# A three-part change to a hybrid decoder layer in fp32 on one core: 1/rms spread by its column, residual rows turned in a later stage by way of HBM, last partial products staged in working buffers

## The chip, the cores and the metric

The kernel runs on one core of a Trainium2 chip. The metric is the device time of one execution in microseconds (us); 843.92 is the median of three runs before the change. The engines are TensorE (PE; its weight loads are shown apart as PEld), VectorE (DVE), ScalarE (ACT), GpSimd (POOL) and SyncE (SP, which here only issues DMAs). Each engine works through its own instructions in the order in which the program holds them; an instruction that waits on a semaphore holds up all that stands behind it on its engine.

## What is computed

One layer: a half-step SwiGLU feed-forward block (FFN), a token mixer, and a second half-step FFN, each with RMSNorm before and after. There are 512 tokens of width 1024, and the FFN's hidden width is 2816 (22 chunks of 128). All is fp32.

```
x = x + 0.5 * rms_norm(swiglu(rms_norm(x, g1), w_gu1, w_down1), g1b)
x = x + rms_norm(hybrid_mixer(rms_norm(x, g2), ...), g2b)
x = x + 0.5 * rms_norm(swiglu(rms_norm(x, g3), w_gu2, w_down2), g3b)

rms_norm(x, g) = x * rsqrt(mean(x * x, -1) + 1e-6) * g
swiglu(x, w_gu, w_down): gate, up = split(x @ w_gu); (silu(gate) * up) @ w_down
```

The mixer joins a gated linear recurrence on half of its channels with sliding-window attention on the other half.

## The kernel before

**Products.** Every fp32 product is made of three: operands are split into a high part (rounded to the matmul's format, by ACT) and a low part (the rest, by DVE), and PE adds high x high, high x low and low x high. Weights go through the same split: a raw tile is loaded on SP's queue, ACT casts it (tiles whi...), DVE subtracts (wlo...). The class Weights does this a fixed number of units ahead of PE (AHEAD, 4), and its calls fix where the casts and subtractions stand in the order of ACT and DVE. `W.later(n, fn)` puts a step n units later.

**The residual stream** xT lies turned: features on the partitions, tokens along them, eight tiles of 128 x 512, in two raw buffers of 1 MB each out of five (NRAW). In the first FFN it is lent to HBM (`lend`, two DMAs of 1 MB on POOL's queue) and fetched back (`give_back`), so that the weights can have its buffers.

**1/rms.** At every RMSNorm the sums of squares are made by PE per half of 256 tokens (`InvRms.stats`, line 550), ACT takes the root (line 556), DVE the reciprocal (line 558): a column of 128 partitions x 2. `invert` then multiplies the identity by that column (dg, line 560, DVE), and `spread` (line 564) multiplies a matrix of ones with dg on PE, which gives 1/rms along the free dimension on all partitions. There are 12 such spreads.

**The second FFN** (loop over GROUPS2 at the end): chunks 0 to 5 are done in the plain way (`classic`); four octos follow, each for four chunks (f0 = 6, 10, 14, 18). `octo` makes gate and up with seven products instead of eight (the forms b11, t3, t2, b21, t1, t4, b22), each of 24 matmuls of 512 columns (line 951), in PSUM banks A, Dd and B, two banks each. The third form, t2, is added to A; the copies u2 (line 956) read A; the fifth, t1, is added to A again. The hidden values are turned by DVE into a tile z (line 961), put to HBM (h_b, line 965, SP's queue) and loaded again (hxb, line 1021, SP's queue) during the next octo, to serve as operands of `seven_down`. `seven_forms_of` hangs these steps on the products of the octo: its dictionary has step numbers as keys, where 1 is the loading of hxb and 2.5 the cast of its first block (line 827, ACT; low part line 834, DVE).

**seven_down** (line 1088 on) makes the down product of the previous octo's chunks, again in seven products (a11, s3, a12, s2, s4, a22, s1). From the second on, each ends in copies of two banks into stage tiles (line 1113, ACT) and accumulating DMAs of 256 KB on POOL's queue into HBM (yp_b, line 1116): 14 a group. A later accumulation to the same place waits until the earlier one has landed. The stage tiles are three acc tiles and one R tile, and then tiles of 2 KB a partition of the pool t2k (38 buffers).

**Pools.** wt gives working tiles (8 buffers), which an octo uses for p1, p7, u4 and its forms s1 to s4; wide gives tiles of 8 KB a partition (2 buffers), used for z and hxb.

**The rows.** The output is by tokens, so xT is turned back: `turn_back(c)` is one DVE transpose (in blocks of 32 x 32, line 1870) and four stores into x_hbm (line 1873, SP's queue), in runs of 32 floats. It runs eight times in `classic` of the second FFN, between the steps 2.5 and 4.5. The rows are loaded in the last group (read_x, line 1918).

Of the kernel before, what the change touches and what calls it, by code (L numbers as in the profile page):

```python
# [15 lines left out]
P = 128  # L16
# [106 lines left out]
def tile_layer(ctx: ExitStack, tc: tile.TileContext, out: bass.AP, **ins: bass.AP):  # L123
# [39 lines left out]
    def wt(name, w=T, dt=F32):  # L163
        return tmp.tile([P, w], dt, tag="w", name=name, bufs=NW)
# [304 lines left out]
    def filled(name, w, value):  # L469
        t = const.tile([P, w], F32, name=name)  # L470
        dve.memset(t, value)
        return t

    ones = filled("ones", P, 1.0)
    mean_d = filled("mean_d", 1, 1.0 / D)
    mean_c = filled("mean_c", 1, 1.0 / C)
    eps = filled("eps", 1, EPS)
# [61 lines left out]
    class InvRms:  # L539
# [13 lines left out]
        def invert(self, ms, scale=1.0):  # L553
            n = self.name
            rms = small.tile([P, 2], F32, tag="rms", name=f"rms_s{n}")
            act.activation(rms, ms, AF.Sqrt, bias=self.eps, scale=scale)
            rs = small.tile([P, 2], F32, tag="rs", name=f"rs_{n}")
            dve.reciprocal(rs, rms)
            self.dg = wt(f"dg_{n}", T)[:, :2 * P].rearrange("p (a b) -> p a b", a=2)
            dve.tensor_tensor(self.dg, ident.unsqueeze(1).to_broadcast([P, 2, P]), rs.unsqueeze(2).to_broadcast([P, 2, P]), op=ALU.mult)  # L560

        def spread(self):
            o = self.ps[:, T // 2:]
            pe.matmul(o, ones, self.dg.rearrange("p a b -> p (a b)"), start=True, stop=True)
            return o


# [231 lines left out]
    class Hidden:  # L799
# [129 lines left out]
            for j in range(2):  # L929
                self.hs[f + j] = hs[j]  # L930

        def octo(self, f, beside, soon=False):


            n = f"{self.name}{f}"

            def did(i):
                for fn in beside.get(i, ()):
                    fn()

            h_hbm = hbm.tile([4 * P, T], F32, name=f"h_{n}")

            def seven(b, form, first, i):
                for q in range(2):
                    hi, lo = W.take(3 if soon and i == 6 and q else AHEAD)
                    for tb in range(2):
                        blk = slice(tb * P, (tb + 1) * P)
                        for k in range(2):
                            xh, xl = self.nxt.t[form, 2 * q + k]
                            for j, (x, w) in enumerate(((xh, hi), (xl, hi), (xh, lo))):  # L950
                                pe.matmul(b[tb], x[:, blk], w[:, k, :], start=first and q + k + j == 0, stop=q + k == 2 and j == 2, skip_group_check=True)  # L951
                    did(i + q / 2)

            def each(fn, *args):
                for xs in zip(*args):
                    fn(*xs)

            def turned(xs, h):

                for tb, x in enumerate(xs):  # L960
                    dve.transpose(z.rearrange("p (j b n) -> p b j n", n=32, b=NB)[:, 2 * h + tb], x.rearrange("p (j n) -> p j n", n=32))

                def put():
                    for i in range(4):
                        sync.dma_start(h_hbm[:, i * P:(i + 1) * P].rearrange("(j a) n -> a j n", a=32), z[32 * i:32 * (i + 1)].rearrange("p (j n) -> p j n", n=P))

                if h:
                    W.later(1, put)

            def pair(make, name):  # L970
                return [make(f"{name}{n}{tb}") for tb in range(2)]

            z = wide(f"z{n}")
            A, Dd, B = (pair(bank, s) for s in "adb")
            p1, p7, u4 = (pair(wt, s) for s in ("p1", "p7", "u4"))
            u2 = pair(acc_tile, "u2")
            g1 = [acc_tile(f"g1{n}0"), r_tile(f"g1{n}1")]
            silu = lambda o, x: act.activation(o, x, AF.Silu)
            add = lambda o, x: dve.tensor_add(o, o, x)
            mul = lambda o, x: dve.tensor_mul(o, o, x)  # L980
            seven(A, "b11", True, 0)
            each(act.copy, B, A)
            seven(Dd, "t3", True, 1)
            each(act.copy, p7, Dd)
            seven(A, "t2", False, 2)
            each(act.copy, u2, A)
            seven(B, "b21", False, 3)
            W.later(1, each, silu, p1, B)
            seven(A, "t1", False, 4)
            each(act.copy, u4, A)  # L990
            W.later(1, each, add, u4, p7)
            seven(Dd, "t4", False, 5)
            each(add, u2, Dd)
            each(mul, u2, p1)
            W.later(1, turned, u2, 0)
            seven(A, "b22", False, 6)
            each(silu, g1, A)
            if soon:
                each(mul, g1, u4)
                turned(g1, 1)  # L1000
            else:
                W.later(1, each, mul, g1, u4)
                W.later(1, turned, g1, 1)
            return h_hbm
# [83 lines left out]
    def seven_down(hid, f, one, part, forms, ahead, beside={}, keep=False):  # L1088

        free = [r_tile] + 3 * [acc_tile]
        for fn in beside.get(-1, ()):
            fn()
        A, B, Dd, E_ = ([bank(f"y{s}{hid.name}{f}{i}") for i in range(2)] for s in "abde")
        for n, (banks, form, blocks) in enumerate(((A, "a11", []), (Dd, "s3", [(1, 1)]), (B, "a12", [(0, 0)]), (A, "s2", [(1, 0)]),
                                    (E_, "s4", [(0, 1)]), (Dd, "a22", [(1, 0)]), (A, "s1", [(1, 1), (0, 1)]))):
            if form == "s3":
                W.fill(AHEAD, True)
                hid.steps.pop(0)()  # L1100
            one(banks, W.take(ahead if form == "a11" else AHEAD), forms[form], form in ("a11", "s3", "s4"))
            if form == "a11":
                for i in range(2):
                    act.copy(B[i], A[i])
            if hid.steps and form != "s3":
                hid.steps.pop(0)()
            for i in range(2 if form in (("s3", "s2") if keep else ("a12", "s3", "s2", "s4", "a22", "s1")) else 0):
                if keep:
                    o = part(*blocks[0], i)
                    dve.tensor_add(o, o, banks[i])  # L1110
                    continue
                st = free.pop()("stage") if free else t2k("stage")
                act.copy(st, banks[i])  # L1113
                for half, dh in blocks:
                    o = part(half, dh, i)
                    pool.dma_start(o, st.rearrange("p (a b) -> p a b", a=2) if len(o.shape) == 3 else st, accum_op=ALU.add)  # L1116
            for fn in beside.get(n, ()):
                fn()
        return {(0, 0): B, (1, 0): Dd, (0, 1): E_, (1, 1): A}
# [68 lines left out]

    warm = bank("warm")

    def spin(n):
        for i in range(n):
            pe.matmul(warm[:, (i % 4) * P:(i % 4 + 1) * P], ident, ident, start=True, stop=True)

    spin(WARM)
    g1_ps = bank("g1_ps")
    tps = turn_early()
    pe.transpose(g1_ps[:, :KD], g1rows, ident[:KD, :KD])
    dve.tensor_copy(g1, g1_ps[:, :KD])
    spin(6)  # L1200
    banks = [bank(f"a_first{i}") for i in range(4)]

    def passes(js, ks, part=0, xpart=0, stop=False):
# [661 lines left out]

    x_hbm = hbm.tile([T, D], F32, name="x_hbm")

    def turn_back(c):
        z = t2k(f"z{c}")
        dve.transpose(z, xT[c])  # L1870
        for i in range(4):
            o = x_hbm[:, c * P + i * 32:c * P + (i + 1) * 32].rearrange("(j a) n -> a j n", a=32)
            sync.dma_start(o, z[32 * i:32 * (i + 1)].rearrange("p (j n) -> p j n", n=32))


    parts = {(tb, dh): hbm.tile([P, T], F32, name=f"yp_b{tb}{dh}") for tb in range(NB) for dh in range(2)}
# [45 lines left out]
    def read_gain():  # L1922
        for dh in range(2):
            grow.append(t2k(f"grow{dh}"))
            sync.dma_start(grow[dh], ins["ffn2_post_g"][0:1, dh * T:(dh + 1) * T].to_broadcast([P, T]))

    last = {-1: [lambda: (read(0, 0), read(0, 1), read(1, 0), read(1, 1), read_gain(), read_x(0))],
            2: [lambda: hid.fetched(f0, h_hbm[f0])], 3: [lambda: read_x(1)], 4: [lambda: (hid.split(f0), hid.split(f0 + 1))]}
    down = lambda half, dh, i: parts[2 * half + i, dh]
    for g, (f0, f1) in enumerate(GROUPS2):  # L1930
        if g:
            h_hbm[f0] = hid.octo(f0, hid.seven_forms_of(before, h_hbm[before], (1, 2.5, 3.5, 4.5, 5.5, 6)), f1 == FC)
            kept = seven_down(hid, before, by_tokens, down, hid.forms, AHEAD - 1, *((last, True) if f1 == FC else ()))
            before = f0
            continue
# [1 line left out]
        spare.extend(fours("hs0", F32R))  # L1937
        held = {f: hid.all_held[:, (f - 2) * T:(f - 1) * T] for f in range(2, f1)}
        h_hbm[2] = None
        turns = [(turn_back, c) for c in range(KD)]  # L1940
        hs = hid.classic(f1, banks, {2: [(n2.sums, 0)], 2.5: [(n2.lows, 0)] + turns[:2], 3: turns[2:4], 3.5: [(n2.sums, 1)] + turns[4:5], 4: [(n2.lows, 1)] + turns[5:7], 4.5: [(n2.sums, 2)] + turns[7:], 5: [(n2.lows, 2)], 5.5: [(n2.sums, 3)]}, AHEAD - 1, held)

        def others(dh, f):
            for fn, k in {(0, 0): [(n2.lows, 3)]}.get((dh, f), ()):
# [100 lines left out]
```

## Time and profile before

| | |
|---|---|
| median of three runs | 843.92 us (843.78 to 845.41) |
| the profiled execution | 843.12 us, of which the profile's span is 841.4 us |
| granted clock of TensorE | 0.998 |
| the first transposes of xT to the last store of the rows | 549.2 to 573.9 us |
| octo of chunk 10, first product to last | 641.10 to 679.65 us |
| octo of chunk 14, first product | 698.69 us |
| stage copies of ACT that waited for a DMA | 5 of 72, 22.1 us |

Times in the profile's rows are us from the start of the span; a row of the timeline or of the chain gives its start, its length, the engine, the line and what it writes and reads, and in brackets how long the engine stood idle before it and for whom. DMA queue q0 holds what POOL issues, q1 what SP issues. A row of a queue gives its packets, its MB, and the time that its packets took as a share of 16 DMA engines; with two queues active the shares of one window can add to a little over 100%.

### The profile page before, as it was taken

How to read it: one execution, taken by the hardware profiler on the slowest of the kernel's cores; microseconds unless marked ns; L12 is line 12 of the kernel's file. 1: busy time of each engine (PE TensorE's matmuls, PEld its weight loads, DVE VectorE, ACT ScalarE, POOL GpSimd, SP SyncE). 2: the span in 40 equal slices, each digit the busy share in tenths (PEclk: the TensorE clock that was granted, in tenths of full speed). 3: DMA queues.
4: the chain of work that ended last, by engine and by line, in shares of the span. 5: the costliest groups of instructions: out<-in, count | busy, mean ns of one | idle time of the engine just before them, and what ended most of it. 6: DMA issues, size and time to landing. Idle time of an engine off the chain costs nothing.

```text
span 841.4 us, 12381 instructions
## 1 busy us (share of the span) xinstructions
PE 832.6 (99%) x4504; PEld 718.5 (85%) x4504; DVE 722.6 (86%) x1026; ACT 519.2 (62%) x821; POOL 163.3 (19%) x178
## 2 busy tenths in 40 slices
PE   9999999999999999999999999999999999999996
PEld 8988888988988998987788899888888888888885
DVE  4978999998979965879889589799998998997996
ACT  6746856666666655556797446536757767666562
POOL 2023000140320333304531052002004113032001
PEclk9999999999999999999999999999999999999999
DMA  7249419398595799223511131169439939769842
GB/s 252 77 131 349 152 59 313 90 249 260 128 247 189 166 261 339 85 73 98 157 51 51 51 115 37 50 140 290 168 108 232 322 87 255 249 149 260 302 140 101
DMA packets 123613, 143.73 MB, mean 171 GB/s; under 512 B 23896, under 2 KB 81568, under 8 KB 123040
## 3 DMA queue, kind: packets, MB, share of 16 engines
q1 hardware_dynamic: 109232, 111.86, 41.9%
q0 software_dynamic: 14176, 30.94, 17.1%
q8 instruction: 35, 0.57, 0.3%
q14 instruction: 26, 0.21, 0.1%
q10 hardware_dynamic: 144, 0.13, 0.0%
HBM read 100.45 MB, written 40.89 MB: 168 GB/s over the span
## 4 chain that ended last, share of the span: by engine, by line
PE 89%; DVE 6%; ACT 2%; DMA 1%; issue 1%; DVEq 0%; POOL 0%; ACTq 0%; POOLq 0%
PE aa L951 10%; PE ab L951 10%; PE da L951 5%; PE db L951 4%; PE yaa L1347 3%; PE bb L951 3%; PE ba L951 3%; PE yda L1347 2%; PE ya L506 2%; PE ya L507 2%; PE ya L508 2%; PE a_first L1206 1%; PE aa L881 1%; PE yab L1884 1%; PE yab L1886 1%; PE yab L1885 1%
## 5 line engine op out<-in xcount | busy, mean ns | idle before, releaser
L1116 POOL DMA_DIRECT2D yp_a<-stage x42 | 36.8, 1079 | 181.3 <-ACT stage L1113 158.8
L1116 POOL DMA_DIRECT2D yp_b<-stage x42 | 36.4, 1078 | 144.7 <-ACT stage L1113 117.8
L506 PE MATMUL ya<-hha,whi_ad 128*128 128x512 f32 x62 | 24.1, 389 | 0.0
L507 PE MATMUL ya<-hla,whi_ad 128*128 128x512 f32 x62 | 24.1, 389 | 0.0
L508 PE MATMUL ya<-hha,wlo_ad 128*128 128x512 f32 x62 | 24.1, 389 | 0.0
L686 POOL TENSOR_TENSOR acca_r<-acca_r,sq_r 128x512 f32<-128x512 f32 x6 | 8.1, 1355 | 62.3 <-ACT sq_r L536 62.3
L1900 POOL DMA_DIRECT2D yp_b<-stage x8 | 4.3, 547 | 67.5 <-ACT stage L1899 67.5
L1113 ACT COPY stage<-yab 128x512 f32<-128x512 f32 x12 | 6.5, 607 | 15.6 <-DMA yp_b<-stage 15.6
L524 PE MATMUL an<-xh_mx,whi_xl 128*128 128x256 f32 x64 | 15.9, 288 | 0.0
L525 PE MATMUL an<-xh_mx,wlo_xl 128*128 128x256 f32 x64 | 15.5, 283 | 0.0
L2000 ACT ACTIVATE ysq<-yp 128x512 f32<-128x512 f32 (+1 forms) x8 | 4.8, 606 | 16.7 <-DVE yp L1993 16.7
L2003 POOL TENSOR_TENSOR last<-yp,grow 128x512 f32<-128x512 f32 x3 | 3.9, 1299 | 57.3 <-DVE yp L1993 57.3
L506 PE MATMUL gt<-xh_mx,whi_gt 128*128 128x512 f32 x32 | 14.3, 445 | 0.0
L508 PEld LDWEIGHTS ya<-hha,wlo_ad 128*128 128x128 f32 x62 | 11.6, 188 | 2.4
L506 PEld LDWEIGHTS ya<-hha,whi_ad 128*128 128x128 f32 x62 | 11.6, 188 | 2.4
L507 PEld LDWEIGHTS ya<-hla,whi_ad 128*128 128x128 f32 x62 | 11.6, 188 | 2.4
L536 ACT ACTIVATE sq_r<-yp_a 128x256 f32<-128x256 f32 (+1 forms) x10 | 5.0, 502 | 12.9 <-DVE yp_a L676 5.9
L506 PE MATMUL pq<-xh_mx,whi_q 128*128 128x512 f32 x32 | 12.8, 399 | 0.0
L506 PE MATMUL pub<-xh_f,whi_bu 128*128 128x512 f32 x32 | 12.6, 395 | 0.0
L508 PE MATMUL gt<-xh_mx,wlo_gt 128*128 128x512 f32 x32 | 12.6, 394 | 0.0
L507 PE MATMUL gt<-xl_mx,whi_gt 128*128 128x512 f32 x32 | 12.6, 393 | 0.0
L506 PE MATMUL pgb<-xh_f,whi_bg 128*128 128x512 f32 x32 | 12.6, 393 | 0.0
(2014 smaller groups left out, 3474.9 us busy)
## 6 DMA issues: line engine op xcount, KB each, us to landing
yp_a<-stage POOLq DMA_DIRECT2D x50, 256.0 KB, 9.0
yp_b<-stage POOLq DMA_DIRECT2D x50, 256.0 KB, 9.1
h_a<-za SPq DMA_DIRECT2D x16, 256.0 KB
hxa<-h_a SPq DMA_DIRECT2D x16, 256.0 KB
h_b<-zb SPq DMA_DIRECT2D x16, 256.0 KB
hxb<-h_b SPq DMA_DIRECT2D x16, 256.0 KB
xn<-in_x SPq DMA_DIRECT2D x8, 256.0 KB
xT_hbm<-xT POOLq DMA_DIRECT2D x2, 1024.0 KB, 9.4
```

The source lines that it names most:

```text
L506: pe.matmul(ps, hi[:, k, :], xh, start=start, stop=False)
L507: pe.matmul(ps, hi[:, k, :], xl, start=False, stop=False)
L508: pe.matmul(ps, lo[:, k, :], xh, start=False, stop=stop)
L524: pe.matmul(ps[:, sl], hi[:, k, :], xh, start=k == 0 and not goes_on, stop=False, skip_group_check=True)
L525: pe.matmul(ps[:, sl], lo[:, k, :], xh, start=False, stop=False, skip_group_check=True)
L881: pe.matmul(o, w[:, k, js], x, start=first and i + j + k == 0, stop=k == 3 and i == 2, skip_group_check=True)
L951: pe.matmul(b[tb], x[:, blk], w[:, k, :], start=first and q + k + j == 0, stop=q + k == 2 and j == 2, skip_group_check=True)
L1116: pool.dma_start(o, st.rearrange("p (a b) -> p a b", a=2) if len(o.shape) == 3 else st, accum_op=ALU.add)
L1206: pe.matmul(banks[j][:, HALF[0]], ws[j][part][:, k, :], n1.xs[k][xpart][:, HALF[0]], start=k == 0 and part == xpart, stop=stop and k == KD ...
L1347: pe.matmul(o, a[:, k, ms], x[:, js], start=first and i + k + m % 2 == 0, stop=k == 1 and i == 2, skip_group_check=True)
L1884: pe.matmul(banks[i], hh[:, js], hi[:, k, :], start=first and k == 0, stop=False, skip_group_check=True)
L1885: pe.matmul(banks[i], hh[:, js], lo[:, k, :], start=False, stop=False, skip_group_check=True)
```

## The change

It has three parts.

1. `invert` ends with the reciprocal. `spread` makes two products instead of one, each with the column of 1/rms, repeated 128 times, as the weights, and the identity as what streams. The tile of ones goes; ident_r, a copy of the identity in the matmul's rounded format, comes, and four more warm-up products use it at the start.
2. In `seven_down` the stage tiles of the last product, s1, come from wt. There are two of them in each call, each read by two accumulating DMAs.
3. The rows are turned later. After the mixer, xT is lent to HBM (two DMAs on POOL's queue). After the octos of chunks 6 and 10, ahead of the seven_down that follows, half of it is fetched (`fetch_back`, one DMA of 1 MB on POOL's queue) into a wide tile. In the octos of chunks 10 and 14, at step 0 (the first half of the first product), four transposes into wt tiles turn that half and 16 stores put it to x_hbm; the wide tile then serves as the octo's z.

As built, on SP's queue of the octos of chunks 10 and 14 the 16 stores stand behind the last raw_by loads and ahead of the four loads of hxb, the raw_bxd and the raw_byd; on DVE the four transposes stand behind the first wlo_br; on POOL's queue the fetch stands ahead of the 14 accumulating stores and waits for the last reads of the tile whose buffer it takes (hla of the form a22).

```diff
-    ones = filled("ones", P, 1.0)
+    ident_r = const.tile([P, P], F32R, name="ident_r")
+    dve.tensor_copy(ident_r, ident)
...
-            rs = small.tile([P, 2], F32, tag="rs", name=f"rs_{n}")
-            dve.reciprocal(rs, rms)
-            self.dg = wt(f"dg_{n}", T)[:, :2 * P].rearrange("p (a b) -> p a b", a=2)
-            dve.tensor_tensor(self.dg, ident.unsqueeze(1).to_broadcast([P, 2, P]), rs.unsqueeze(2).to_broadcast([P, 2, P]), op=ALU.mult)
+            self.rs = small.tile([P, 2], F32, tag="rs", name=f"rs_{n}")
+            dve.reciprocal(self.rs, rms)
 
         def spread(self):
             o = self.ps[:, T // 2:]
-            pe.matmul(o, ones, self.dg.rearrange("p a b -> p (a b)"), start=True, stop=True)
+            for i in range(2):
+                pe.matmul(o[:, i * P:(i + 1) * P], self.rs[:, i:i + 1].to_broadcast([P, P]), ident, start=True, stop=True)
             return o
...
-        def octo(self, f, beside, soon=False):
+        def octo(self, f, beside, soon=False, rows=None):
...
-            z = wide(f"z{n}")
+            z = wide(f"z{n}") if rows is None else rows[1]
+            if rows is not None:
+                beside = {0: [lambda: turn_back(*rows)], **beside}
...
-                st = free.pop()("stage") if free else t2k("stage")
+                st = (wt if form == "s1" else free.pop() if free else t2k)("stage")
...
-    spin(WARM)
+    spin(WARM, ident)
...
-    spin(6)
+    spin(6, ident)
+    spin(4, ident_r)
...
-    def turn_back(c):
-        z = t2k(f"z{c}")
-        dve.transpose(z, xT[c])
-        for i in range(4):
-            o = x_hbm[:, c * P + i * 32:c * P + (i + 1) * 32].rearrange("(j a) n -> a j n", a=32)
-            sync.dma_start(o, z[32 * i:32 * (i + 1)].rearrange("p (j n) -> p j n", n=32))
+    def fetch_back(half):
+
+        x = wide(f"xT_back{half}")
+        pool.dma_start(x, xT_hbm[half])
+        return half, x
+
+    def turn_back(half, x):
+
+        for j in range(KD // 2):
+            c, z = half * KD // 2 + j, wt(f"z{half}{j}")
+            dve.transpose(z, x[:, j * T:(j + 1) * T])
+            for i in range(4):
+                o = x_hbm[:, c * P + i * 32:c * P + (i + 1) * 32].rearrange("(j a) n -> a j n", a=32)
+                sync.dma_start(o, z[32 * i:32 * (i + 1)].rearrange("p (j n) -> p j n", n=32))
...
-            h_hbm[f0] = hid.octo(f0, hid.seven_forms_of(before, h_hbm[before], (1, 2.5, 3.5, 4.5, 5.5, 6)), f1 == FC)
+            h_hbm[f0] = hid.octo(f0, hid.seven_forms_of(before, h_hbm[before], (1, 2.5, 3.5, 4.5, 5.5, 6)), f1 == FC, rows)
+            rows = fetch_back(g - 1) if g < 3 else None
...
-        turns = [(turn_back, c) for c in range(KD)]
-        hs = hid.classic(f1, banks, {2: [(n2.sums, 0)], 2.5: [(n2.lows, 0)] + turns[:2], 3: turns[2:4], 3.5: [(n2.sums, 1)] + turns[4:5], 4: [(n2.lows, 1)] + turns[5:7], 4.5: [(n2.sums, 2)] + turns[7:], 5: [(n2.lows, 2)], 5.5: [(n2.sums, 3)]}, AHEAD - 1, held)
+        lend(x_tiles)
+        hs = hid.classic(f1, banks, {2: [(n2.sums, 0)], 2.5: [(n2.lows, 0)], 3.5: [(n2.sums, 1)], 4: [(n2.lows, 1)], 4.5: [(n2.sums, 2)], 5: [(n2.lows, 2)], 5.5: [(n2.sums, 3)]}, AHEAD - 1, held)
```

More of the change, by code (lines that the diff above doesn't have):

```diff
@@ L1189, in tile_layer, with spin @@
     warm = bank("warm")
-    def spin(n):
+    def spin(n, w):
         for i in range(n):
-            pe.matmul(warm[:, (i % 4) * P:(i % 4 + 1) * P], ident, ident, start=True, stop=True)
-    spin(WARM)
+            pe.matmul(warm[:, (i % 4) * P:(i % 4 + 1) * P], w, w, start=True, stop=True)
+    spin(WARM, ident)
     g1_ps = bank("g1_ps")
@@ L1925, in read_gain @@
             sync.dma_start(grow[dh], ins["ffn2_post_g"][0:1, dh * T:(dh + 1) * T].to_broadcast([P, T]))
+    rows = None
     last = {-1: [lambda: (read(0, 0), read(0, 1), read(1, 0), read(1, 1), read_gain(), read_x(0))],
```

## Prediction

> **What bounds the kernel now.** First the page's head, its busy times and its chain, then what TensorE (PE) waited for.
>
> ```profile
> span 841.4 us, 12381 instructions
> PE 832.6 (99%) x4504; PEld 718.5 (85%) x4504; DVE 722.6 (86%) x1026; ACT 519.2 (62%) x821; POOL 163.3 (19%) x178
> PE 89%; DVE 6%; ACT 2%; DMA 1%; issue 1%; DVEq 0%; POOL 0%; ACTq 0%; POOLq 0%
> PE warm L1193 <- POOL ident masks.py:199: 1.4, 1, 1.4
> PE g_ps L1198 <- DMA rows<-in_ffn_pre_g: 0.4, 1, 0.4
> PE rms_lru L550 <- DVE acc_lru L1800: 0.3, 1, 0.3
> ```
>
> PE is busy 99% of the span and waits 2.1 us in all, nowhere near this change. So there is next to nothing to win, and what counts is whether anything begins to stop PE. The chain, by stretches, shows PE's products of one octo (the second FFN's block of seven products, 24 matmuls each) and the two places where PE lost a little.
>
> ```profile
> 594.02 0.49 ACT bb L956
> 594.56 5.74 PE ab L951 x24
> 652.11 5.78 PE ab L951 x24
> 657.89 5.44 PE bb L951 x24
> 663.33 5.44 PE ab L951 x24
> 720.45 5.44 PE ab L951 x24
> ```
>
> A product takes 5.44 us; those at 594.56 and 652.11 took 0.3 more, because ScalarE (ACT) was late. That 0.6 us is all that freeing ACT and VectorE (DVE) can return.
>
> **Part 1: 1/rms spread by the column.** Two rows of weight loads (PEld) from the timeline, and the removed operation.
>
> ```profile
> 533.36 0.85 PEld L564 LDWEIGHTS rms_nf<-dg_nf,ones 128*128 128x128 f32 x4
> 5.96 1.41 PEld L1193 LDWEIGHTS warm<-ident 128*128 128x128 f32 x12
> L560 DVE TENSOR_TENSOR dg_r<-ident,rs_r x4: 425/425/459, 342.7 to 508.4; 128x256 f32<-128x256 f32 x4
> 7.73 0.19 PEld L1206 LDWEIGHTS a_first<-xh_a,whi_first 128*128 128x128 f32 x1 [0.18 <-ACT xh_a L580]
> ```
>
> One spread was two passes, 0.85/4 = 0.21 us each, 0.43 in all. It becomes two products of 128 columns, four passes. The warm-up products have just that form: 1.41/12 = 0.12 each, 0.47. So 0 to +0.05 each, 12 spreads: I take **+0.5 us** on PE (bounds 0, and +1.6 at a stall of 0.13 each for weights read from one repeated column, which no row shows). DVE loses 12 x 0.43 = 5.1 us, worth nothing, since PE waits at no spread. The four extra warm-up products (0.5 us by the same rate) end before the fourth matmul that waits for ACT's xh_a: the three waits of 0.18 cover all but the last tenths. 0.
>
> **Part 2: last copies in working buffers.** ACT, DVE and PE in the first products of the octo of chunk 10.
>
> ```profile
> 648.61 1.08 ACT L1113 COPY stage<-yab 128x512 f32<-128x512 f32 x2 [5.15 <-DMA yp_b<-stage]
> 645.22 1.22 DVE L289 TENSOR_TENSOR wlo_br__6665<-raw_bx__6369,whi_br__6664 128x1024 fp32r<-128x1024 f32 x1
> 646.35 1.22 DVE L296 TENSOR_TENSOR raw_bx__6369<-raw_bx__6369 128x1024 f32<-128x1024 f32 x1
> 650.66 1.23 DVE L289 TENSOR_TENSOR wlo_br__6708<-raw_bx__6387,whi_br__6707 128x1024 fp32r<-128x1024 f32 x1 [3.10 <-ACT whi_br__6707 L285]
> 655.46 0.39 PE L951 MATMUL ab<-wlo_br__6708,t24h_f 128*128 128x512 f32 x1
> ```
>
> ACT stood 5.15 us until an accumulating store gave a 2 KB buffer back, and DVE 3.10 us behind it. With a working buffer both go; PE gets back the 0.3 of 652.11. In the first FFN the same wait cost PE nothing. What is late next: the working buffers come free only when the last four accumulating stores land, and DVE's s3b and ACT's p1b of the next octo take them; part 3 settles that.
>
> **Part 3: the rows turned later.** It leaves the first group of the second FFN: eight transposes, 32 stores on SP's queue. It comes back as two 1 MB writes (DMA idle there), and in the octos of chunks 10 and 14 as one 1 MB fetch on POOL's queue, four transposes and 16 stores on SP's queue.
>
> ```profile
> L1870 DVE STREAM_TRANSPOSE z<-xT x8: 667/698/705, 549.2 to 571.2; 128x512 f32<-128x512 f32 x8
> 549.95 9.33 SPq L1873 DMA_DIRECT2D x_hbm<-z  x16
> 559.38 5.36 DMA raw_bd<-in_ffn_w_down
> 634.91 3.22 SPq L1021 DMA_DIRECT2D hxb<-h_b  x4
> 634.10 0.68 DVE L834 TENSOR_TENSOR hla<-u,hha 128x512 fp32r<-128x512 f32 x1
> 633.50 1.79 POOL L1116 DMA_DIRECT2D yp_b<-stage  x2 [46.23 <-ACT stage L1113]
> 657.22 0.63 ACT L827 CAST hha<-hxb 128x512 fp32r<-128x512 f32 x1
> 657.73 1.09 ACT L956 COPY u2b<-ab 128x512 f32<-128x512 f32 x2
> 713.85 0.65 ACT L827 CAST hha<-hxb 128x512 fp32r<-128x512 f32 x1
> ```
>
> *The group left*: PE was short only at 594.56; with 8 x 0.61 us less on DVE and SP free sooner for raw_bd, that goes: **-0.3 us**.
> *The transposes*: they stand behind the wlo_br of 645.22, in the hole that part 2 empties; 4 x 0.62 = 2.5 us against 3.10 (loss if that cover goes: 2.5 us a time, less the lead of wlo_br, which ends at 651.9 and is first read at 655.46). 0.
> *The stores* are the point. The last rows are SP's and ACT's, that of raw_bd one of the chain (from its issue to its use). SP issues in order. Before, the four loads of hxb went out at 634.91, 22 us ahead of ACT's cast of 657.22. Now 16 stores stand ahead of them, and wait for the transposes (z ready at 647 to 649), then take 9.33 us to issue: hxb goes out at about 657. Behind them wait raw_bxd too. Behind ACT's cast, in ACT's own order, stand the copies u2b, which empty the bank that PE's product of 663.33 writes. So hxb must land by 663.33 - 0.5 - 0.5 = **662.3**, or PE stops.
>
> How long the stores take depends on who else is on the DMA engines. Their queues, by windows: 641 to 648; 637 to 638; 549 to 562 (the stores alone); 632 to 676; and the 1 MB fetches of the first FFN, 327 to 345.
>
> ```profile
> q0 software_dynamic: 566, 1.03, 79.7%
> q1 hardware_dynamic: 562, 0.62, 31.1%
> ...
> q0 software_dynamic: 26, 0.05, 31.1%
> ...
> q1 hardware_dynamic: 8506, 1.29, 56.5%
> ...
> q0 software_dynamic: 2016, 3.67, 45.6%
> ...
> q0 software_dynamic: 288, 2.10, 28.1%
> ```
>
> In the first window both queues had work: 566 packets against 562 at different sizes. The engines take **one packet from each queue in turn** (POOL's accumulating stores on q0, SP's transfers on q1). The turned stores are 512 packets of 128 B each, 8192 an octo, against 2016 on q0 for the whole stage. In turn with q0 they hardly move until q0 is empty, and hxb is queued behind them. So hxb waits for all of it: 14 accumulating copies, 45.6% of 44 = 20.1 us of all engines; the fetch, 28.1% of 18 halved = 2.5; the stores, 56.5% of 13 = 7.3 with a little of another load, I take 7; the rest of raw_by, about 1. Sum 30.6; the shares add to 1.11 where the engines are full, so 27.6 us. q0 starts at about 638.3: the fetch waits for the last read of its buffer (hla of 634.10, to 634.8) and the first packets came 3.5 us after an issue (633.50; the 26 of 637 to 638 are q0's first). 638.3 + 27.6 + 1 of gap while POOL waits for stores to land = 666.9. The first load of hxb needs, by estimate, 2.6 more (raw_bd, four times that size, took 5.36 from issue to use): it **lands at 669.5**. ACT casts (0.5) and copies (0.5, and 0.1 to PE), and PE goes on at 670.6 instead of 663.33: **+7.3 us**. The 0.3 of 652.11 is in this figure, as PE would have been there 0.3 sooner. In chunk 14's octo everything stands 57.1 us later by PE (720.45) and 56.6 by ACT's cast (713.85): 6.8 to 7.3, I take **+7.3 us** again. Bounds for each: 0 (hxb in time) and +11 (stores and fetch wait 2 to 3 us more, as when the fetch lands late and delays the transposes). I take the value nearest to the 641 to 648 rows.
>
> The rest follows: s3b and p1b find their buffers free by then; hxb's reader being late, DVE falls some 2 us further behind PE, which its lead covers.
>
> **Sum**: +0.5 - 0.3 + 7.3 + 7.3 = +14.8 on the span, 856.2; outside it the profiled run has 843.12 - 841.4 = 1.7: 857.9; that run is 0.8 under the median of the three: **858.7**.
>
> **Rivals.**
> *A: equal time, not equal packets.* If the engines give each queue half of their time, the stores' 7 us take 14/1.11 = 12.6 from about 649.5, the first hxb lands at 664.7, PE loses 2.5 twice: with +0.5 - 0.3 that is **849**. Against it: 566 to 562 packets, though their shares were 79.7 and 31.1%. [...]
> *B: not slower.* The stores run as they did alone (9.33 us to issue, landed soon after), hxb goes out at 657 and lands by 660. It decides at 662.3. Then only +0.5 - 0.6 is left: **843.8**. For it: unmixed, 8448 packets took 56.5% of 13 us. Against: q0 is busy in the whole stretch.
> *C: DVE becomes the bound*: the fetch comes so late that the transposes start after 649; wlo_br then stops PE, about 1.5 us in each octo, hxb in time: **847**.
> *D: longer*: raw_byd and raw_bxd, queued behind hxb, stop ACT a second time ahead of the u4 copies that PE needs two products later, some 4 us an octo: **867**.
>
> **How the numbers follow.** Forecast 0.62 (852 to 866), A 0.12 (846 to 852), B 0.18 (842 to 845), C 0.05, D 0.03. A measurement of this kernel tells some 0.2%, 1.7 us, from no change. Slower: 0.62 + 0.12 + 0.05 + 0.03 = 0.82; B gives 0.15 within and 0.03 faster. The range 844.5 to 866 leaves out most of B, and D, under 0.2.
>
> **What would show it.** Right: in both octos ACT waits some 13 us for DMA hxb ahead of its first cast, PE waits 7 to 8 us for ACT's u2b, q0 and q1 show equal packet counts from about 650, and the ACT wait of 5.15 is gone. The spread's loads run at 0.12 us. Wrong: hxb landed by 662 of the old time base, q1 far ahead of q0 in packets; or a PE wait at wlo_br.

## The result and the profile after

The changed kernel takes 862.16 us, median of four runs (861.77 to 862.8), beside 844.1 for the kernel before (four runs too, 843.78 to 845.41): 1.0215 times as long, 95% interval 1.0203 to 1.0227, so 18 us more. The profiled execution has a span of 860.8 us, 19.4 over that of before. First the page's head and its queues (packets, MB, share of the 16 DMA engines), then PE's and ACT's longest waits (us in all, times, longest).

```profile
span 860.8 us, 12422 instructions
PE 839.0 (97%) x4532; PEld 723.8 (84%) x4532; DVE 719.0 (84%) x1014; ACT 520.1 (60%) x821; POOL 165.2 (19%) x182
q1 hardware_dynamic: 109232, 111.86, 40.8%
q0 software_dynamic: 14752, 35.14, 18.0%
```

```profile
PE ab L951 <- ACT u2b L956: 12.8, 2, 7.9
ACT hha L827 <- DMA hxb<-h_b: 25.0, 2, 14.0
```

PE, which waited 2.1 us in all before, now waits 12.8 us in two places for the u2b copies, and ACT waits 25.0 us in two places for hxb. That is the chain of the forecast. The chain's links in the octo of chunk 10, from SP's, ACT's and PE's timelines, and SP's rows of the octo of chunk 14:

```profile
645.10 18.51 SPq L1884 DMA_DIRECT2D x_hbm<-z  x16
663.71 2.00 SPq L1023 DMA_DIRECT2D hxb<-h_b  x4
666.65 0.62 ACT L827 CAST hha<-hxb 128x512 fp32r<-128x512 f32 x1 [10.98 <-DMA hxb<-h_b]
667.17 1.07 ACT L956 COPY u2b<-ab 128x512 f32<-128x512 f32 x2
667.81 0.80 PE L951 MATMUL ab<-whi_bt__6736,t13h_f 128*128 128x512 f32 x1 [4.89 <-ACT u2b L956]
712.11 19.49 SPq L1884 DMA_DIRECT2D x_hbm<-z  x16
731.64 2.04 SPq L1023 DMA_DIRECT2D hxb<-h_b  x4
```

SP needs 18.5 and 19.5 us to issue 16 stores which took 9.33 before the change; hxb goes out behind them, ACT's cast, which stood 10.98 us for it, starts at 666.65, and the u2b copies and PE's product follow within 1.2 us.

A second loss stands in the rows behind the two waits: first the matmuls behind the first wait, then TensorE's granted clock (PEclk, the third column from the end) in a stretch without a wait and in the 6 us behind each wait.

```profile
668.40 0.63 PE L951 MATMUL ab<-whi_bt__6736,t13l_f 128*128 128x512 f32 x1
668.83 0.63 PE L951 MATMUL ab<-wlo_bt__6737,t13h_f 128*128 128x512 f32 x1
```

```profile
630.00:636.00 6.00, 6.00 (x28) 4.96 (x27) 6.00 (x7) 6.00 (x10) 1.33 (x3) 1.00 0.92 239
667.60:673.70 6.10, 5.89 (x14) 4.65 (x15) 5.33 (x7) 5.08 (x8) 0.00 (x0) 0.50 0.99 347
735.80:741.80 6.00, 5.83 (x14) 4.63 (x15) 5.22 (x7) 5.04 (x8) 0.00 (x0) 0.50 1.00 348
```

Behind each wait PE runs at half its clock for some 6 us: a matmul starts every 0.43 us and not every 0.23 (5.44 / 24), so 14 or 15 are made where 26 were possible. Half of 6 us is 3 us lost each time. So 12.8 us of waiting and 6 us of half clock make 18.8 of the 19.4.

### The profile page after: what moved, and what is told of

Its sections match the earlier page's. It is cut to its first block, busy times and chain, and to the rows that moved or that the text cites. A ratio compares the mean times of both kernels' runs of the same rounds, so it can differ in the third digit from the quotient of the medians.

```text
span 860.8 us, 12422 instructions
## 1 busy us (share of the span) xinstructions
PE 839.0 (97%) x4532; PEld 723.8 (84%) x4532; DVE 719.0 (84%) x1014; ACT 520.1 (60%) x821; POOL 165.2 (19%) x182
## 3 DMA queue, kind: packets, MB, share of 16 engines
q1 hardware_dynamic: 109232, 111.86, 40.8%
q0 software_dynamic: 14752, 35.14, 18.0%
## 4 chain that ended last, share of the span: by engine, by line
PE 80%; DVE 10%; issue 4%; SPq 2%; DMA 2%; ACT 2%; DVEq 0%; ACTq 0%
PE aa L951 10%; PE da L951 5%; PE ab L951 5%; PE yaa L1350 3%; PE ba L951 3%; PE yda L1350 2%; PE db L951 2%; PE ya L507 2%; PE ya L508 2%; PE ya L509 2%; SPq L1884 1%; PE aa L881 1%; PE a_first L1209 1%; DMA raw_byd__6778<-in_ffn_w_down 1%; PE yea L1350 1%
## 5 line engine op out<-in xcount | busy, mean ns | idle before, releaser
L834 DVE TENSOR_TENSOR hla<-hxb,hha 128x512 fp32r<-128x512 f32 x9 | 6.2, 688 | 26.3 <-ACT hha L827 26.3
L827 ACT CAST hha<-hxb 128x512 fp32r<-128x512 f32 x9 | 5.5, 615 | 25.0 <-DMA hxb<-h_b 25.0
L507 PE MATMUL pq<-xh_mx,whi_q 128*128 128x512 f32 x32 | 12.8, 400 | 0.0
L537 ACT ACTIVATE sq_r<-yp_a 128x256 f32<-128x256 f32 (+1 forms) x10 | 5.0, 503 | 12.8 <-DVE yp_a L676 5.9
L827 ACT CAST hhs<-s4b 128x512 fp32r<-128x512 f32 x4 | 2.5, 623 | 16.8 <-DVE s4b L863 16.8
```

Source lines behind the costliest of these rows:

```text
L507: pe.matmul(ps, hi[:, k, :], xh, start=start, stop=False)
```

## The experiments

Each run was compared with runs of the kernel before in the same session; the ratios are to those.

**1. hxb ahead of the stores.**

```diff
-                beside = {0: [lambda: turn_back(*rows)], **beside}
+                beside = {0: beside[1] + [lambda: turn_back(*rows)], **{k: v for k, v in beside.items() if k != 1}}
```

> The changed kernel with one thing moved: in the octos of chunks 10 and 14 the four loads of hxb stand ahead of the 16 stores of x_hbm on SP's queue, not behind them. Theory (the stores, held back by POOL's accumulating copies, hold back hxb): both waits of PE for u2b go (4.9 and 7.9 us), and with them the stretches of half clock behind them (2.8 and 3.0 us): 862.2 - 13 - 6 = 843.4, plus 0 to 4 if raw_byd, still behind the stores, now stops ACT ahead of the u4 copies. So 843 to 847. Rival (the small stores slow everything in that stage, whatever the order): hxb lands late as before, 858 or more. Rival (ACT is stopped a second time by raw_byd, forecast rival D): a wait of PE for u4b of about 4 us in each octo, with a slow clock again, about 855.

861.74 us, 1.0217 (1.0203 to 1.0231): no gain. SP's, ACT's and PE's rows of the octo of chunk 10; then PE's longest wait:

```profile
634.90 2.69 SPq L1023 DMA_DIRECT2D hxb<-h_b  x4
645.36 23.50 SPq L1884 DMA_DIRECT2D x_hbm<-z  x16
670.04 0.92 SPq L175 DMA_DIRECT2D raw_byd__6778<-in_ffn_w_down  x2
676.03 1.04 ACT L318 CAST whi_bdp__6863<-raw_byd__6778 128x1024 fp32r<-128x1024 f32 x1 [10.22 <-DMA raw_byd__6778<-in_ffn_w_down]
678.13 0.79 PE L951 MATMUL ab<-whi_bv__6815,b2h_f 128*128 128x512 f32 x1 [4.06 <-ACT u4b L956]
```

```profile
PE ab L951 <- ACT u4b L956: 10.4, 2, 6.4
```

The wait for u2b is gone and the next one in SP's queue has taken its place: raw_byd goes out at 670.0 (at 658.98 in the kernel before), ACT stands 10.2 us for it ahead of the u4b copies, and PE waits 10.4 us in the two octos together, again with a slower clock behind each wait (0.51 and 0.69 in the next 6 us). This is the mechanism of the prediction's rival D, here in place of the first wait instead of on top of it. The expectation had it as its second rival, at about 855; the theory's 843 to 847 is missed. I had taken 18.5 us of issue as given, and it became 23.5. The 1 MB of hxb now went out ahead of the stores, and the accumulating copies were through later: ACT's p1b waited for one until 664.72, where in the changed kernel q0 had 3 packets left after 660.7. So it isn't the place of hxb that costs but 16 stores that block SP's queue for 18 to 24 us.

**2. Without the third part.** The loop and `turn_back` of the kernel before, with parts 1 and 2 kept.

> The changed kernel without its third part: the rows are turned and stored in the first group of the second FFN, as before the change; parts 1 and 2 stay. Theory (all of the loss is part 3): within 1 us of the kernel before, 843.5 to 845, the stall of 0.3 us at the product of 652.11 gone, ACT's wait of 5.15 us gone. Rival (the spread by a repeated column costs 0.13 us a time, or the working buffers given to s1 are missed later): 845.5 or more, with a new wait of PE, DVE or ACT for a stage or s3b tile.

843.19 us, 0.9997 (0.9988 to 1.0005), 0.3 under the expected range. All of the loss is part 3: 862.16 - 843.19 = 19 us. PE waits 1.7 us in all.

**3. The first part alone.**

```diff
-            pe.matmul(o, ones, self.dg.rearrange("p a b -> p (a b)"), start=True, stop=True)
+            for i in range(2):
+                pe.matmul(o[:, i * P:(i + 1) * P], self.rs[:, i:i + 1].to_broadcast([P, P]), ident, start=True, stop=True)
```

> The kernel before with the first part of the change alone. Forecast of the prediction: 0.5 us slower (0 to 1.6), 843.9 to 845.5. Rival: the loads of a repeated column are no slower than others and DVE's 5 us less bring PE nothing: 843.9, within 0.2. What is read first is the time of the weight loads of the spread in the timeline: 0.12 us each by the forecast, 0.21 or more by its upper bound.

842.82 us, 0.9991 (0.9982 to 1.0000): no loss that a measurement can tell, and 1.1 us under the expected range. The spread's loads and ACT's wait in the timeline, then two rows of the chain:

```profile
533.88 1.08 PEld L564 LDWEIGHTS rms_nf<-ident,rs_nf 128*128 128x128 f32 x8
647.63 1.08 ACT L1115 COPY stage<-yab 128x512 f32<-128x512 f32 x2 [4.74 <-DMA yp_b<-stage]
```

```profile
595.03 5.44 PE ab L951 x24
652.15 5.44 PE ab L951 x24
```

Two spreads are eight loads in 1.08 us, against four in 0.85: 0.115 us more for one spread, 1.4 for 12 at most (by the starts of the matmuls around them it is 0.06 where two stand together, 0.12 for a single one, and 0.8 for all 12). Most of it comes back: the two products that took 0.3 us too long before (594.56 and 652.11) take 5.44 here. ACT's wait for a stage tile is still there, 4.74 instead of 5.15; whether these 0.4 us are what put ACT in time isn't shown.

**4. Work in the waits of PE.**

```diff
+                if rows is not None and i == 3:
+                    for q, (hi, lo) in enumerate(taken):
...
+                                    pe.matmul(Dd[tb], x[:, blk], w[:, k, :], start=q + k + j == 0, stop=q + k == 2 and j == 2, skip_group_check=True)
```

> The changed kernel with 48 matmuls more: in the octos of chunks 10 and 14 the product b21 is made a second time, into banks that the next product but one overwrites (so nothing of the output changes), just where PE stands waiting for u2b. It puts 5.44 us of work into each wait. Theory (a PE that has stood still for some us runs at half clock for the next 6 us): in the first octo the wait is filled but for 0.4 us of overhang and the slow stretch goes, -2.4; in the second 2.5 us of wait are left, and the slow stretch goes (-3.0) if that is too short for it, or stays (0). So 856.8 to 860. Rival (the half clock has another cause, such as the loads that come at that moment): no slow stretch less, 862.2 to 863.

Its expectation is wrong in one point: t4 is added to those banks, which hold t3, so the second b21 stands in t3's place in the hidden values of chunks 10 to 17. 861.74 us, 1.0217 (1.0203 to 1.0230): the expected 2 to 5 us did not come. The granted clock did answer. PE's two waits, and the 6 us behind each:

```profile
669.72 0.50 PE L953 MATMUL ab<-whi_bt__6736,t13h_f 128*128 128x512 f32 x1 [0.49 <-ACT u2b L966]
735.90 0.63 PE L953 MATMUL ab<-whi_bt__7286,t13h_f 128*128 128x512 f32 x1 [2.23 <-ACT u2b L966]
```

```profile
669.70:675.70 6.00, 5.98 (x26) 4.98 (x27) 5.21 (x7) 4.91 (x7) 0.00 (x0) 1.00 1.01 347
735.90:741.90 6.00, 6.00 (x19) 4.78 (x20) 5.22 (x7) 4.88 (x7) 0.00 (x0) 0.72 1.02 365
```

At the same place, with the same loads arriving (DMA share 1.01, 347 GB/s), a PE that waited 0.49 us keeps its full clock where one that waited 4.89 us fell to 0.50; after 2.23 us it falls to 0.72. So it is the standing still. By the starts of its matmuls PE does win 1.8 and 1.5 us on the changed kernel in the two octos, as much as was expected. Of these 3.3 us it loses 1.1 again in the seven_down behind the first octo, and 0.8 in the last group, where it waits for hla. Another 0.9 us was lost ahead of the first octo, where the two kernels are the same: that is scatter. Of the time that PE alone won, 0.4 us is left in the result (862.16 against 861.74).

**5. Without the accumulating copies beside the stores.**

```diff
+                    if hid.name == "b" and f in (2, 6):
+                        continue
                     o = part(half, dh, i)
                     pool.dma_start(o, st.rearrange("p (a b) -> p a b", a=2) if len(o.shape) == 3 else st, accum_op=ALU.add)
```

> The changed kernel without the 28 accumulating copies of the two seven_down ahead of the octos of chunks 10 and 14 (the products of chunks 2 to 9 are left out of the sum in HBM, so the output lacks them). The 16 stores, their order and the transposes stay; what goes is the work of POOL's queue beside them. Theory (the stores crawl because the queue of the accumulating copies has packets ready): SP issues the 16 in some 9 to 10 us, as it did alone before the change (9.33), hxb goes out at about 655 and lands by 659, PE doesn't wait: 842 to 844. Rival (the stores take 18 us of their own in this stage): hxb still lands after 663, 858 to 862.

The products of chunks 2 to 9 are left out of the sum in HBM. 843.35 us, 0.9991 (0.9981 to 1.0001). SP's rows, and the DMA queue in 8 us of the stores:

```profile
645.87 8.54 SPq L1886 DMA_DIRECT2D x_hbm<-z  x16
654.50 2.00 SPq L1023 DMA_DIRECT2D hxb<-h_b  x4
```

```profile
q1 hardware_dynamic: 7692, 0.95, 75.4%
```

The same 16 stores at the same time take 8.5 us when POOL's queue is empty, 18.5 when it is full, and the whole loss is gone. In the changed kernel, by the queues in 652 to 660 and in 661 to 664, when q0 had run dry:

```profile
q0 software_dynamic: 800, 1.47, 100.1%
q1 hardware_dynamic: 1623, 0.20, 21.8%
...
q1 hardware_dynamic: 3305, 0.41, 87.4%
```

Beside q0 the stores get 1623 / 8 = 203 packets a us; alone 3305 / 3 = 1100 (962 in the run without accumulation). By the shares, 100.1 against 21.8%, POOL's queue had most of the engines' time. And the 203 are a mean of two states. The same queues of the changed kernel in 657.5 to 658 and in 659 to 660:

```profile
q0 software_dynamic: 45, 0.07, 78.2%
q1 hardware_dynamic: 233, 0.03, 44.1%
...
q0 software_dynamic: 104, 0.19, 104.0%
q1 hardware_dynamic: 104, 0.01, 16.7%
```

Where q0 fills the engines (104.0%), a packet of one queue goes for a packet of the other, 104 to 104; most of the stores get through where q0 is short of packets (233 in half a us beside 45 of q0's).

**6. The same bytes in long runs.**

```diff
-                o = x_hbm[:, c * P + i * 32:c * P + (i + 1) * 32].rearrange("(j a) n -> a j n", a=32)
-                sync.dma_start(o, z[32 * i:32 * (i + 1)].rearrange("p (j n) -> p j n", n=32))
+                r = (c * P + i * 32) // 2
+                sync.dma_start(x_hbm[r:r + 16].rearrange("a (b t) -> (a b) t", b=2), z[32 * i:32 * (i + 1)])
```

> The changed kernel with the same 16 stores of 64 KB at the same places, but each row of the turned tile goes out as one run of 2 KB, 32 packets a store and not 512 (the rows lie wrong in HBM, so the output is wrong). Theory (what is dear is the number of packets, each in turn with one of the other queue): 512 packets an octo beside some 90 a us of the other queue are gone in 6 us, hxb goes out by 655 and lands by 659, no wait for u2b: 842 to 845. Rival (the dear part is that hxb waits behind the transposes and behind 16 issues, whatever they carry): hxb at 655 to 660 or later, a wait of PE of 2 us or more in each octo, 850 or more.

The rows then lie in another order in HBM. 853.24 us, 1.0110 (1.0091 to 1.0128), from two runs: half of the loss is left. The time is the rival's (850 or more); its wait of 2 us or more came in one octo alone (4.3 us, and 1.1 in the other). SP's rows and ACT's cast:

```profile
645.74 9.19 SPq L1884 DMA_DIRECT2D x_hbm<-z  x16
655.40 2.67 SPq L1023 DMA_DIRECT2D hxb<-h_b  x4
663.53 0.62 ACT L827 CAST hha<-hxb 128x512 fp32r<-128x512 f32 x1 [7.24 <-DMA hxb<-h_b]
```

With 32 packets a store SP is through in 9.2 us, so the number of packets makes the other 9. But the first load of hxb, the 256 KB that the cast reads, is issued at 655.4 and there only at 663.5, 8.1 us later, beside a q0 whose packets took 71.5% of the engines in 655 to 664 (q1's 39.6%). In the changed kernel, with q0 dry, it took 2.9 us (663.71 to 666.65). Two things cost, then: the small packets, and that hxb is issued 20 us later than it was, into the same crowd (PE waits 5.5 us, and 6 us at a granted clock of 0.54, a loss of 2.8 us, follow the longer of the two waits).

**7. All of the turning later.**

```diff
-                beside = {0: [lambda: turn_back(*rows)], **beside}
+                beside = {**beside, 4.5: [lambda: turn_back(*rows)] + beside.get(4.5, [])}
...
-            c, z = half * KD // 2 + j, wt(f"z{half}{j}")
+            c, z = half * KD // 2 + j, t2k(f"z{half}{j}")
```

> The changed kernel with the turning (four transposes and 16 stores) at a later place in the same octos: at step 4.5, behind the loads of hxb, raw_bxd, raw_byd and raw_bx on SP's queue, when the accumulating copies have all landed; the turned tiles come from t2k. Theory: the stores take 9 to 10 us of issue, nothing that is wanted soon stands behind them, no wait for u2b or u4b: 842.5 to 844, by the 0.6 of the first part less than the kernel before at best. Rival (the later place delays raw_by and the h_b put behind it, or 2.5 us of DVE there hit a short lead): a new wait of PE of 1 us or more in the next octo, 845 to 850.

845.14 us, 1.0012 (1.0003 to 1.0021): 17 us of the 18 are back; 1 to 2 us over parts 1 and 2 alone remain. That is the rival's time, though PE has no new wait of 1 us.

**8. Half of it later.** Two tiles are turned and stored at step 0 (js 0 and 1, in wt), two at step 4.5 (js 2 and 3, in t2k).

> As the run with the turning at step 4.5, but only half of it is moved: two transposes and eight stores stay ahead of hxb. Theory (the stores go at a fraction of a packet to a packet of the other queue until that is empty, at 660.5, and hxb can't land before some 3 us later unless they are through): eight stores have 4096 packets, and some 3500 went by 660 in the changed kernel: hxb goes out at 660 and lands at 663, PE waits about 1 us in the first octo and 2 to 4 in the second, with little of the slow clock: 845 to 851. Rival (the wait goes with the number of stores): half of 13 us, and the slow clock in both octos: 855.

853.98 us, 1.0120 (1.0106 to 1.0134), 3 us over the expected range and 1 under the rival's. SP's rows, and PE's longest wait:

```profile
645.11 9.35 SPq L1884 DMA_DIRECT2D x_hbm<-z  x8
654.56 5.68 SPq L1023 DMA_DIRECT2D hxb<-h_b  x4
```

```profile
PE ab L951 <- ACT u2b L956: 4.9, 2, 3.6
```

Eight stores take 9.35 us, where hxb was expected to go out only 15 us after their start, but behind them the four issues of hxb take 5.68 beside q0 instead of 2. Neither the end of q0 alone nor the number of stores alone sets the wait: hxb is held up in the same crowd as the stores.

**9. Transposes early, stores late.** As 7, but the four transposes stay at step 0 and only the stores go to 4.5, there behind the step's own work (in 7 ahead of it); the turned tiles lie in t2k in between.

> All three parts of the change, with the transposes where the changed kernel has them (step 0, in the hole that DVE has there) and the 16 stores at step 4.5, as in the run that moved both. The turned tiles come from t2k, since they now live 25 us longer. Theory (the stores ahead of hxb cost the 18 us, and the 2 us that were left when both were moved are DVE's 2.5 us of transposes in a stage where PE is close behind DVE): no wait of PE for u2b, u4b or hla: 842.8 to 843.8, as the kernel without the third part (843.2). Rival (what was left came from the stores at the later place, which hold up the loads of raw_by or the h_b put): 844.8 to 845.5, as with both moved.

844.61 us, 1.0006 (0.9997 to 1.0014): between the two expectations. In 7 and 9 SP still takes 13.6 and 15.6 us for 16 stores, now among the loads of its own queue, and the turned tiles hold buffers of t2k that ACT's casts want. ACT's waits of 7, then of 9:

```profile
ACT hha L827 <- DMA x_hbm<-z: 3.1, 2, 1.9
```

```profile
ACT hha L827 <- DMA x_hbm<-z: 4.0, 2, 2.8
```

By the starts of PE's matmuls, beside those of experiment 2, the rest of the loss arises in the three seven_down behind the octos of chunks 10, 14 and 18: some 0.4, 0.8 and 1.0 us in 7, and 0.6, 0.3 and 0.9 in 9. PE's waits there are small, 0.4 to 0.6 us for hla and twice 0.2 for a bank that ACT copies. That ACT's waits for the stores are what makes them isn't shown.

**10. The stores on POOL's queue.**

```diff
-            c, z = half * KD // 2 + j, wt(f"z{half}{j}")
+            c, z = half * KD // 2 + j, t2k(f"z{half}{j}")
...
-                sync.dma_start(o, z[32 * i:32 * (i + 1)].rearrange("p (j n) -> p j n", n=32))
+                pool.dma_start(o, z[32 * i:32 * (i + 1)].rearrange("p (j n) -> p j n", n=32))
```

> The changed kernel with the 16 stores at their place, but issued by POOL, on the queue of the accumulating copies and behind the 14 of them, and not on SP's; the turned tiles come from t2k. Theory (the loss is made by what stands behind the stores on SP's queue, not by the small packets on the engines as such): hxb, raw_bxd and raw_byd go out in time, the stores go when the accumulating copies are through, from 660 to 672 or so, nothing waits for them: 842.8 to 844. Rival (small packets from whatever queue slow the loads beside them): raw_byd of the octo, loaded at that time, lands late, and PE waits for u4b by 1 to 4 us in each octo: 846 to 855. Rival (POOL takes long to issue 512 packets and holds up the next fetch): the fetch and the transposes after it late, DVE late: 845 to 848.

842.64 us, 0.9983 (0.9974 to 0.9992), 1.5 us under the kernel before. PE waits 1.7 us in all. The run changes two things at once, the queue and, as the last section shows, the number of packets; fewer packets alone left half of the loss (experiment 6). It and the kernel of experiment 2 were measured once more together:

> The kernel with the 16 stores on POOL's queue once more, in one call with the kernel without the third part, to see what the third part is worth once its stores stand in nobody's way. Theory (it is worth the 0.3 us of the first group and no more, so the 1.5 us measured before were mostly parts 1 and 2 and the chip's scatter): 0.0 to 0.6 us below the kernel without the third part. Rival (the whole 1.5 us is the third part): 1 us or more below it.

> The kernel with parts 1 and 2 alone once more, beside the one with the stores on POOL's queue. Theory: 0.4 to 1.2 us below the kernel before, as measured before (0.6), and 0.0 to 0.6 above the other. Rival: no difference to the kernel before, and 1 us or more above the other.

843.13 us, 0.9994 (0.9985 to 1.0003), and 843.35, 0.9995 (0.9986 to 1.0004). The 1.5 us were probably scatter for the most part: in the two sessions the change with its stores on POOL's queue is 0.17 and 0.06% faster than before, the second time with no difference inside the interval, and it is 0.2 us from parts 1 and 2 alone. Another queue cures the loss; a gain behind it can't be measured.

## Why the prediction was right, point by point

**What bounds the kernel** held: PE, and what stops it. **The spread** was put at +0.5 us and costs 0.8 to 1.4 by its rows, inside the bounds of 0 to 1.6; the time doesn't show it. The 0.13 us a spread of the upper bound was the author's guess; experiment 3's loads took 0.115 more for one spread. **The two hiccups of 0.3 us** went, as forecast, but not for the causes given: they are gone with part 1 alone, while the first group's turning and ACT's wait for a stage tile are still there. Parts 1 and 2 together are within 0.2% of nothing (0.9995 to 0.9997).

**The transposes** cost nothing, as worked out: DVE's rows show them in the hole that part 2 empties, and the second wlo_br, which stands behind them, ends at 649.1 and is first read by PE at 655.0.

```profile
643.24 1.22 DVE L289 TENSOR_TENSOR wlo_br__6613<-raw_bx__6315,whi_br__6612 128x1024 fp32r<-128x1024 f32 x1
644.37 2.48 DVE L1881 STREAM_TRANSPOSE z<-xT_back 128x512 f32<-128x512 f32 x4
...
647.88 1.22 DVE L289 TENSOR_TENSOR wlo_br__6655<-raw_bx__6333,whi_br__6654 128x1024 fp32r<-128x1024 f32 x1
```

**The stores** are the step that made the forecast, and the mechanism is the one that runs 1, 2, 5 and 10 show: stores held back by POOL's queue, hxb behind them, ACT behind hxb, PE behind ACT. Its size was 7.3 + 7.3 us of waiting; it is 4.9 + 7.9. In the first octo hxb landed at 666.65 and not at 669.5: q0 had already moved 0.24 MB by 638, where I let it start at 638.3, and the rest of the sum was a little long. In the second octo I moved the whole stage by 57 us and took the same loss. That failed because the fetch there waits for something else:

```profile
633.92 0.55 POOL L1874 DMA_DIRECT2D xT_back<-xT_hbm  x1 [48.42 <-ACT stage L1115]
700.94 0.57 POOL L1874 DMA_DIRECT2D xT_back<-xT_hbm  x1 [46.97 <-DMA h_b<-xT_back]
```

The second fetch needs the wide tile that the octo of chunk 10 used as z, and so the end of the h_b puts: it goes out 5.2 us ahead of the octo's first product (706.12) and the first one 7.1 us ahead (640.99). All of q0's work and the stores behind it come 2 us later against PE, and the issues of the stores take 1 us longer (19.5 against 18.5): that is the difference between waits of 4.9 and 7.9. That the two misses, 2.4 too much and 0.6 too little, partly cancel is luck.

**One packet from each queue in turn** held where q0 kept all engines full: 104 to 104 in the us shown in experiment 5. The equal counts from about 650 on, which were to show the forecast right, did not come for the whole stretch (1623 against 800 in 652 to 660), because q0 was short of packets in between and the stores passed then. Equal time, by which rival A lived, it was not (104.0 against 16.7% of the engines). The forecast didn't hang on the exact ratio: all but 3 of q0's packets had gone by 660.7 and hxb went out at 663.71, so all of the work was done before hxb even so.

**The term that was missing** is the half clock, 3 us behind each wait, 6 in all. The forecast of 858.7 is 3.5 us under the measured 862.2: 6 us of clock left out, 1.8 us of waiting too many (14.6 against 12.8), and about 1 us of parts 1 and 2 forecast too dear (+0.2 against -0.6). So two errors of opposite sign stand in a number that looks near. The trace before shows no such wait: PE's longest is 1.4 us, at the start, and the granted clock of the first 13 us is 1.00. In the changed kernel the slow clock came behind both waits, of 4.9 and 7.9 us, and on it matmuls of 512 columns start 0.43 us apart (668.40 and 668.83). With the 3 us that the rows show behind each, a wait of 7.3 us would have been priced at 10.3.

**The rivals.** A (849) and B (843.8) fell with the late landing of hxb; C did not occur. D's second stop of ACT by raw_byd is in the changed kernel as a wait of 2.1 us that PE doesn't feel, and came out in full only where hxb was moved ahead. That the next one in the queue takes over was priced too low there: at 0 to 4 us by the theory of experiment 1, where PE waited 4.1 and 6.4 us with a slower clock behind both.

## What to carry to other kernels

Before transfers are put into an in-order queue, count their packets, find what the other queues are doing at that time, and look at everything that stands behind them, not only at the first: here moving hxb away just handed the wait to raw_byd (4.1 and 6.4 us of PE), and another queue cured it (ratios 0.9983 and 0.9994). A stop of a busy PE of 2.2 us or more cost 1.7 to 3 us more than its length here, in all seven cases. A number that comes out near is to be taken apart by its terms before it is believed.

## What the runs showed of the hardware

**The price of a wait of PE.** The granted clock in the 6 us behind ten waits of five kernels (the changed one, and those of experiments 1, 4, 6 and 8), as in the rows above:

| wait of PE, us | 0.49 | 1.14 | 1.27 | 2.23 | 3.64 | 4.06 | 4.32 | 4.89 | 6.39 | 7.93 |
|---|---|---|---|---|---|---|---|---|---|---|
| experiment | 4 | 6 | 8 | 4 | 8 | 1 | 6 | changed | 1 | changed |
| clock, next 6 us | 1.00 | 1.00 | 1.00 | 0.72 | 0.72 | 0.51 | 0.54 | 0.50 | 0.69 | 0.50 |

Behind the waits of up to 1.27 us nothing is lost; behind those from 2.23 us on, 1.7 to 3 us (6 x (1 - clock)), and the loss doesn't follow the length of the wait. None of the ten lies between the two.

**POOL's queue made few packets of the small runs.** The queue rows of the page of experiment 10, to be held against those of the changed kernel above:

```profile
q1 hardware_dynamic: 92336, 109.76, 40.3%
q0 software_dynamic: 15776, 37.24, 19.1%
```

The 32 stores, 2.1 MB in runs of 128 B, took 16,896 packets on SP's queue (109232 - 92336) and take 1,024 on POOL's (15776 - 14752): the same transfer, to the same addresses, in one sixteenth of the packets. With 2.10 MB on either queue (111.86 - 109.76, 37.24 - 35.14), that is 124 B a packet on SP's and 2.05 KB on POOL's, on average. POOL's way of issuing them, 0.65 us a store, showed no cost in the two runs that have it (experiment 10 and its repeat).
